# Attention queries projected by token halves, the second half woven with the attention, query loads on SyncE's queue

## Chip, core and metric

The kernel runs on one core of a Trainium2 chip. The metric is the device time of one execution in microseconds (us). PE is TensorE, PEld its weight loads, DVE VectorE, ACT ScalarE, POOL GpSimd and SP SyncE, which here only issues DMAs.

## What is computed

One encoder block over 1024 tokens of width 1024, float32. Both mixers read the same normalised input through one projection; the attention takes its first 768 columns (512 of queries, 128 of keys, 128 of values).

```python
xn = _rmsnorm(h, norm_mix_w[l])
proj = xn @ w_in[l]
q_a, k_a, v_a, qkv_g, z_g, a_g, b_g = jnp.split(proj, SPLIT_POINTS, axis=-1)
attn = _windowed_gqa(q_a, k_a, v_a, band_bias, in_window, attn_sink[l])   # 8 heads, 2 kv heads, window 128
gdn = _gdn_mixer(qkv_g, z_g, a_g, b_g, conv_w[l], gdn_a_log[l], gdn_dt_bias[l], gdn_norm_w[l])
h = h + jnp.concatenate([attn, gdn], axis=-1) @ w_out[l]
hn = _rmsnorm(h, norm_ffn_w[l])
h = h + jnp.square(jax.nn.relu(hn @ w_ffn_in[l])) @ w_ffn_out[l]
return _rmsnorm(h, norm_final_w)
```

Attention works by blocks of 128 queries (`n`, 0 to 7) against the block before, their own and the next. The second mixer is a gated delta rule in both directions, with a triangular inversion per chunk of 128 tokens.

## The kernel before, in words

Every float32 product of the projections is made of three matmuls: weight and input are each split into a rounded part and a remainder (`split`, L119 on ACT and L120 on POOL), and `mm3` (L124 to L126) adds high by high, high by low, low by high. A `gemm` takes 128 weight columns against 512 tokens: 8 slices of the inner dimension, 24 matmuls. The normalised, transposed and split input is held as `xt[0]` (tokens 0 to 511) and `xt[1]` (tokens 512 to 1023), eight tiles of the tag `pg` each. `pg` has 28 buffers, `sc` and `wr` 4, `wh` and `wl` (split weights) 3, `pt` 12; the PSUM tags `psA` and `psB` have 4 banks each. A tile that finds no buffer waits until an earlier one is read for the last time.

Work is written as generators that yield an estimate of what they have issued. `weave` takes the next piece from the stream whose sum of estimates, divided by its weight, is smallest, and so fixes the written order of instructions. The framework then takes that order as priority and lays out the order of each engine at compile time; on the chip each engine runs its own list in order.

First stage (about 90 to 333 us of the profiled execution): `proj_conv` for v, `proj_z` and `proj_attn` are woven with `prep`, `eliminate`, `diag_blocks` and `invert` for its first two steps (0 and 1):

```python
run(weave((chain(self.proj_conv(C_GV, "v"), self.proj_z(), self.proj_attn()), 145.0),
          (chain(self.prep(), self.eliminate(0), self.diag_blocks(0), self.eliminate(1), self.diag_blocks(1),
                 self.invert(tt, (0, 1))), 100.0)))
self.bias_table()
```

At its end `proj_attn` projects the queries: for each of two kv heads it loads 256 columns, and `pair` runs four gemms: the first half of the tokens for two column tiles, then the second half for both. Each result is scaled on DVE (L492), rounded on ACT (L493), its remainder taken on POOL (L494), and both parts are stored to the DRAM scratch `qad` by four DMAs on SP (L498). `bias_table` loads the four bias tiles (L527, SP).

Second stage (about 333 to 570 us): `output`, which begins with `attention`, is woven with `invert` steps 2 and 3 and then two scans of eight steps each:

```python
run(weave((output(), 100.0),
          (chain(self.invert(tt, (2, 3)), self.scan(0, tt[0], w_attn), self.load_wout(0, (2,)),
                 self.scan(1, tt[1], w_gdn)), 95.0)))
```

`attention` has 16 steps (block `n`, kv head). A step makes scores (`attn_scores`, L542 and L543 on PE, L544 on DVE, L556 on ACT, L561 on DVE and POOL), issues the query load for the step two later (`query`, L592, from POOL's queue), and then closes the step two before it: transposes (L571), copies (L573), and after each second step the product with the values (L583, L586) and a store to `mad` (L587, SP). The queries of the first two steps are loaded in `proj_attn`.

`invert` is a chain through POOL (memset of its target, L708), ACT (L712, L721, L742, L753), PE (L718, L728, L732, L751, L759) and DVE (L737, L744, L762), with its input `atd` loaded on SP (L705). `invert` 2 and 3 take one target each from `wh` and `wl`, the others from `pg`. `eliminate(1)` and `diag_blocks(1)` use `sc`; the latter's two tiles are read by all four inversions. Each scan step takes two `sc` tiles, loads `kvd` (L788), `pd` (L790) and, every second step of the first scan, `ktd` and `qtd` (L778) on SP, and makes its products at L795.

Of the kernel before, what the change touches and what calls it, by code (L numbers as in the profile page):

```python
# [9 lines left out]
F32 = mybir.dt.float32  # L10
F32R = mybir.dt.float32r
BF16 = mybir.dt.bfloat16
AF = mybir.ActivationFunctionType
ALU = mybir.AluOpType
AX = mybir.AxisListType

P = 128
# [3 lines left out]
NK = D // P  # L21
HALF = 512
# [32 lines left out]
def weave(*streams):  # L55

    live = [[0.0, i, g, w] for i, (g, w) in enumerate(streams)]
    while live:
        s = min(live, key=lambda e: (e[0], e[1]))
        try:  # L60
            v = next(s[2])
            s[0] += v / s[3]
            yield v
        except StopIteration:
            live.remove(s)
# [12 lines left out]
class Block:  # L78
# [167 lines left out]
    def w_cols(self, w, c0, n):  # L246
        return lambda kh: [(slice(0, n), w[kh * 512:(kh + 1) * 512, c0:c0 + n].rearrange("(k p) c -> p k c", p=P))]

    def split_w(self, raws, view):
        h, l = self.wh((P, NK, P)), self.wl((P, NK, P))  # L250
        for kh in range(2):
            self.split(view(raws[kh]), h[:, 4 * kh:4 * kh + 4, :], l[:, 4 * kh:4 * kh + 4, :])
        return h, l
# [206 lines left out]
    def proj_attn(self):  # L460


        nc = self.nc
        w = self.io["w_in"][0]
        raws = self.load_w(self.w_cols(w, C_AK, 256))
        lo, up = slice(0, 64), slice(64, 128)
        self.kh, self.kl = [self.pg(dt=F32R) for _ in range(2)], [self.pg(dt=F32R) for _ in range(2)]
        for v, o in enumerate((up, lo)):
            nc.vector.tensor_copy(out=self.kl[v][o, :], in_=self.zero[o, :].to_broadcast([64, SEQ]))
        self.va = self.pg((P, NT, P))  # L470
        for i, half, ps in self.pair(raws):
            tok = slice(half * HALF, (half + 1) * HALF)
            t = self.pt()
            nc.vector.tensor_copy(out=t, in_=ps)
            if i == 0:
                swap = self.pt()
                nc.sync.dma_start(out=swap[up, :], in_=t[lo, :])
                nc.sync.dma_start(out=swap[lo, :], in_=t[up, :])
                for v, (r, o) in enumerate(((lo, up), (up, lo))):
                    nc.scalar.copy(out=self.kh[v][r, tok], in_=t[r, :])  # L480
                    nc.scalar.copy(out=self.kh[v][o, tok], in_=swap[o, :])
                    nc.gpsimd.tensor_tensor(out=self.kl[v][r, tok], in0=t[r, :], in1=self.kh[v][r, tok].bitcast(F32),
                                            op=ALU.subtract)
            else:
                pv = self.transposed(t, 0)
                nc.vector.tensor_copy(out=self.va[:, 4 * half:4 * half + 4, :], in_=pv)
            yield 5.2
        for kv in range(2):
            raws = self.load_w(self.w_cols(w, C_AQ + 256 * kv, 256))
            for i, half, ps in self.pair(raws):  # L490
                q, qh = self.pt(), self.pt(dt=F32R)
                nc.vector.tensor_scalar(out=q, in0=ps, scalar1=0.125, scalar2=None, op0=ALU.mult)  # L492
                nc.scalar.copy(out=qh, in_=q)  # L493
                nc.gpsimd.tensor_tensor(out=q, in0=q, in1=qh.bitcast(F32), op=ALU.subtract)  # L494
                for part, t in enumerate((qh.bitcast(F32), q)):
                    o = 64 * (kv ^ part)
                    for g in range(2):
                        nc.sync.dma_start(out=self.qad[kv, 2 * i + g, o:o + 64, half * HALF:(half + 1) * HALF],  # L498
                                          in_=t[64 * g:64 * g + 64, :])
                if i == 1 and half == 0:  # L500
                    self.qs.append(self.query(0, kv))
                yield 5.2


    def bias_rows(self):
# [83 lines left out]
    def query(self, n, kv):  # L589

        q = self.pt((P, 4, P), F32R)
        self.nc.gpsimd.dma_start(out=q, in_=self.qad[kv, :, :, n * P:(n + 1) * P].rearrange("g c t -> c g t").bitcast(F32R))  # L592
        return q

    def attention(self):

        steps = [(n, kv) for n in range(NT) for kv in range(2)]
        qs = self.qs
        open_, pts = [], []

        def close():
            n, kv, tiles, kbs = open_.pop(0)
            pts.append(self.attn_transpose(tiles, kbs))
            yield 1.3
            if kv == 1:
                self.attn_value(n, pts[:], kbs)
                pts.clear()
                yield 2.6

        for i, (n, kv) in enumerate(steps):  # L610
            mk = self.pg if i % 3 == 2 else self.wr
            open_.append((n, kv, *self.attn_scores(n, kv, self.small((P, 4), tag="nm", bufs=12), qs.pop(0), mk)))
            if i + 2 < len(steps):
                qs.append(self.query(*steps[i + 2]))
            yield 1.3
            if len(open_) > 2:
                yield from close()
        while open_:
            yield from close()
# [634 lines left out]
    def phases(self):  # L1254
        nc = self.nc
# [28 lines left out]
        tt = [[None] * 4, [None] * 4]  # L1284
        self.ct, self.ctt = [None, None], [None, None]
        self.kc, self.qc = [None] * 4, [None] * 4
        self.qs = []
        self.wo, self.hnt, self.scanned, self.summed, self.rows = [{}, {}], [None, None], set(), [], {}
        run(weave((chain(self.proj_conv(C_GV, "v"), self.proj_z(), self.proj_attn()), 145.0),
                  (chain(self.prep(), self.eliminate(0), self.diag_blocks(0), self.eliminate(1), self.diag_blocks(1),  # L1290
# [4 lines left out]
        cols, rest = {}, {}  # L1295

        def output():
            yield from self.attention()
            yield from self.out_attn()
            cols[0], rest[0] = self.columns(self.load_w1(0), 1)  # L1300
            out = self.out_all(range(NT - 1, -1, -1))
            while len(self.summed) < 4:
                yield next(out)
            yield from weave((out, 20.0), (self.tokens_second(), 9.0))

        w_attn = {3: self.load_wout(0, (0,)), 5: self.load_wout(0, (1,)), 7: self.load_wout(0, (3,))}
        w_gdn = {1: self.load_wout(1, (0,)), 2: self.load_wout(1, (1, 2)), 4: self.load_wout(1, (3,))}
# [3 lines that stand above are left out]
# [5 lines left out]
        steps = [(n, p) for n in range(ng // 4) for p in SECOND]  # L1316
# [61 lines left out]
```

## Time and profile before

| | |
|---|---|
| median of 3 runs | 1251.35 us (1249.99 to 1251.94) |
| the profiled execution | 1248.56 us |
| its span | 1246.8 us |
| mean granted clock of TensorE | 0.98 |
| busy: PE, DVE, ACT, POOL | 1184.7, 854.8, 620.7, 577.9 us |

All views are of the one profiled execution. Times in them are microseconds from the start of the span. A row of the timeline gives start, duration, engine, source line, operation, the tile written and the tiles read, and in brackets how long the engine had been idle and what ended that. A row of the waits gives who waited for whom, the sum, the number of times and the longest. The granted clock is a share of TensorE's full clock.

### The profile page before, as it was taken

What the parts mean: (1) busy time and instruction counts of PE and PEld (TensorE: products, weight loads), DVE (VectorE), ACT (ScalarE), POOL (GpSimd) and SP (SyncE); (2) the same over time, 40 slices, a digit from 0 to 9 for tenths busy, and PEclk for the clock granted to TensorE, in tenths of its full rate; (3) what the DMA queues carried; (4) which work ended last, traced back from release to release, by engine and by line L of the source; (5) the groups of instructions that cost most, each with busy time, mean ns of one, the idle gap of its engine ahead of it and who ended that gap; (6) DMA issues with size and microseconds to landing.
All of it is one profiled execution on the core that took longest, in us unless ns stands there. A gap on an engine that the chain in (4) does not pass through costs nothing. (4 is left out here: it accounts for less than half of the span.)

```text
span 1246.8 us, 18527 instructions
## 1 busy us (share of the span) xinstructions
PE 1184.7 (95%) x6482; PEld 968.6 (78%) x6482; DVE 854.8 (69%) x1528; ACT 620.7 (50%) x1347; POOL 577.9 (46%) x488
## 2 busy tenths in 40 slices
PE   7999999899789989998899999999999999999997
PEld 5788877778568868877788888888777888888885
DVE  5677667982389986676645453544669797886976
ACT  6455688345485752125464554545545433444343
POOL 5354211352432333244564535535455555655595
PEclk9999999899889999999999999999999999999999
DMA  6134444341855668122234444443688624444333
GB/s 240 52 121 137 114 157 148 132 127 43 228 169 156 185 219 296 60 85 86 84 120 158 145 153 144 150 165 134 226 284 282 230 85 158 152 125 146 98 89 135
DMA packets 121630, 187.62 MB, mean 150 GB/s; under 512 B 11043, under 2 KB 64416, under 8 KB 121537
## 3 DMA queue, kind: packets, MB, share of 16 engines
q1 hardware_dynamic: 96708, 152.58, 37.6%
q10 hardware_dynamic: 16381, 29.67, 6.2%
q0 software_dynamic: 8448, 4.20, 1.8%
q8 instruction: 51, 0.84, 0.3%
q14 instruction: 42, 0.34, 0.1%
HBM read 122.39 MB, written 63.49 MB: 149 GB/s over the span
## 5 line engine op out<-in xcount | busy, mean ns | idle before, releaser
L124 PE MATMUL psA<-pg,wh 128*128 128x512 f32 x416 | 166.4, 401 | 2.1 <-ACT pt L456 2.1
L126 PE MATMUL psA<-pg,wl 128*128 128x512 f32 x416 | 165.7, 398 | 0.0
L125 PE MATMUL psA<-pg,wh 128*128 128x512 f32 x416 | 165.3, 397 | 0.0
L120 POOL TENSOR_TENSOR wl<-wr,wh 128x512 fp32r<-128x512 f32 x44 | 69.4, 1600 | 153.0 <-ACT wh L119 152.9
L1152 DVE TENSOR_TENSOR pg<-pg 128x512 fp32r<-128x512 f32 x112 | 123.1, 1133 | 19.5 <-ACT pg L1151 19.5
L120 POOL TENSOR_TENSOR wh<-wr,wh 128x512 fp32r<-128x512 f32 x32 | 47.7, 1511 | 129.1 <-ACT wh L119 129.1
L125 PE MATMUL psA<-pg,pg 128*128 128x512 f32 x256 | 99.8, 391 | 0.4 <-POOL pg L120 0.4
L124 PE MATMUL psA<-pg,pg 128*128 128x512 f32 x256 | 99.0, 391 | 1.1 <-DVE pg L1197 0.9
L126 PE MATMUL psA<-pg,pg 128*128 128x512 f32 x256 | 99.7, 389 | 0.0
L1069 ACT ACTIVATE pt<-pt 128x512 f32<-128x512 f32 x64 | 40.4, 631 | 117.6 <-DVE pt L1059 117.6
L120 POOL TENSOR_TENSOR pg<-wr,pg 128x512 fp32r<-128x512 f32 x48 | 73.4, 1558 | 50.8 <-ACT pg L119 50.8
L124 PEld LDWEIGHTS psA<-pg,wh 128*128 128x128 f32 x416 | 79.5, 191 | 19.9 <-ACT pt L456 2.4
L125 PEld LDWEIGHTS psA<-pg,wh 128*128 128x128 f32 x416 | 79.4, 191 | 18.4 <-issue 0.9
L126 PEld LDWEIGHTS psA<-pg,wl 128*128 128x128 f32 x416 | 79.4, 191 | 16.9
L1151 ACT CAST pg<-pg 128x512 fp32r<-128x512 f32 x112 | 66.8, 620 | 42.0 <-DMA pg<-sd 30.3
L125 PE MATMUL psB<-pg,pg 128*128 128x512 f32 x192 | 75.0, 391 | 0.8 <-POOL pg L120 0.7
L126 PE MATMUL psB<-pg,pg 128*128 128x512 f32 x192 | 75.0, 390 | 0.3 <-DVE pg L1152 0.3
L124 PE MATMUL psB<-pg,pg 128*128 128x512 f32 x192 | 74.7, 390 | 0.3 <-ACT pg L1151 0.3
L119 ACT CAST wh<-wr 128x512 fp32r<-128x512 f32 x76 | 43.6, 623 | 43.9 <-PE psA L125 24.3
L1059 DVE TENSOR_TENSOR pt<-psB,pt 128x512 f32<-128x512 f32 x39 | 26.9, 690 | 56.0 <-PE psB L126 29.9
L1059 DVE TENSOR_TENSOR pt<-psA,pt 128x512 f32<-128x512 f32 x39 | 26.8, 689 | 54.0 <-PE psA L126 38.8
L124 PEld LDWEIGHTS psA<-pg,pg 128*128 128x128 f32 x256 | 48.0, 188 | 12.7 <-DVE pg L1197 2.2
(385 smaller groups left out, 3303.7 us busy)
## 6 DMA issues: line engine op xcount, KB each, us to landing
sd<-pt ACTq DMA_DIRECT2D x112, 256.0 KB, 2.1
pg<-sd SPq DMA_DIRECT2D x112, 256.0 KB, 2.9
wr<-in_w_ffn_in SPq DMA_DIRECT2D x32, 512.0 KB, 3.7
wr<-in_w_in SPq DMA_DIRECT2D x22, 512.0 KB, 5.4
pg<-in_x SPq DMA_DIRECT2D x16, 512.0 KB, 4.9
wr<-in_w_ffn_out SPq DMA_DIRECT2D x16, 512.0 KB, 5.1
sc<-kvd SPq DMA_DIRECT2D x14, 512.0 KB, 6.4
kvd<-pt SPq DMA_DIRECT2D x16, 256.0 KB, 2.6
```

The lines of the kernel that those rows point to most:

```text
L119: nc.scalar.copy(out=h, in_=raw)
L120: (eng or nc.gpsimd).tensor_tensor(out=l, in0=raw, in1=h.bitcast(F32), op=ALU.subtract)
L124: nc.tensor.matmul(ps, wh, xh, start=first, stop=False, skip_group_check=onto)
L125: nc.tensor.matmul(ps, wh, xl, start=False, stop=False, skip_group_check=onto)
L126: nc.tensor.matmul(ps, wl, xh, start=False, stop=last, skip_group_check=onto)
L1059: self.nc.vector.tensor_tensor(out=out, in0=in0, in1=in1, op=ALU.add)
L1069: self.nc.scalar.activation(out=c, in_=c, func=AF.Relu)
L1151: nc.scalar.copy(out=s[:, 0], in_=raw)
L1152: v.tensor_tensor(out=s[:, 1], in0=raw, in1=s[:, 0].bitcast(F32), op=ALU.subtract)
```

## The change

`proj_attn` now makes only the gemms of the first half of the tokens, for all four column tiles, and keeps the split weights: three pairs in `wh` and `wl`, the fourth in two `sc` buffers. The four gemms of the second half move to a new generator `proj_late`, woven inside `output` with `attention` at weights 30 to 20; `attention` issues no query load of blocks 4 to 7 before `proj_late` has issued all of its stores. The query of block 0 is loaded after both column tiles of its kv head. `query` is issued by SP instead of POOL.

```diff
-    def split_w(self, raws, view):
-        h, l = self.wh((P, NK, P)), self.wl((P, NK, P))
+    def split_w(self, raws, view, tags=None):
+        hi, lo = tags or (self.wh, self.wl)
+        h, l = hi((P, NK, P), F32R), lo((P, NK, P), F32R)
...
+        self.qw = {}
         for kv in range(2):
             raws = self.load_w(self.w_cols(w, C_AQ + 256 * kv, 256))
-            for i, half, ps in self.pair(raws):
-                q, qh = self.pt(), self.pt(dt=F32R)
...
-                if i == 1 and half == 0:
-                    self.qs.append(self.query(0, kv))
+            for i in range(2):
+                tags = (self.sc, self.sc) if kv and i else (self.wh, self.wl)
+                self.qw[kv, i] = self.split_w(raws, lambda r: r[:, :, i * P:(i + 1) * P], tags)
+                self.store_query(kv, i, 0)
                 yield 5.2
+            self.qs.append(self.query(0, kv))
+
+    def store_query(self, kv, i, half):
+        nc = self.nc
+        ps = self.gemm(self.qw[kv, i], self.xt[half], "psA")
+        q, qh = self.pt(), self.pt(dt=F32R)
+        nc.vector.tensor_scalar(out=q, in0=ps, scalar1=0.125, scalar2=None, op0=ALU.mult)
+        nc.scalar.copy(out=qh, in_=q)
+        nc.gpsimd.tensor_tensor(out=q, in0=q, in1=qh.bitcast(F32), op=ALU.subtract)
+        for part, t in enumerate((qh.bitcast(F32), q)):
+            o = 64 * (kv ^ part)
+            for g in range(2):
+                nc.sync.dma_start(out=self.qad[kv, 2 * i + g, o:o + 64, half * HALF:(half + 1) * HALF],
+                                  in_=t[64 * g:64 * g + 64, :])
+
+    def proj_late(self):
+        for kv in range(2):
+            for i in range(2):
+                self.store_query(kv, i, 1)
+                yield 5.2
+        self.late = True
...
     def query(self, n, kv):
         q = self.pt((P, 4, P), F32R)
-        self.nc.gpsimd.dma_start(out=q, in_=self.qad[kv, :, :, n * P:(n + 1) * P].rearrange("g c t -> c g t").bitcast(F32R))
+        self.nc.sync.dma_start(out=q.bitcast(F32), in_=self.qad[kv, :, :, n * P:(n + 1) * P].rearrange("g c t -> c g t"))
         return q
...
             if i + 2 < len(steps):
+                while steps[i + 2][0] * P >= HALF and not self.late:
+                    yield 0.5
                 qs.append(self.query(*steps[i + 2]))
...
-        self.qs = []
+        self.qs, self.late = [], False
...
-            yield from self.attention()
+            yield from weave((self.proj_late(), 30.0), (self.attention(), 20.0))
```

More of the change, by code (lines that the diff above doesn't have):

```diff
@@ L487, in proj_attn @@
             yield 5.2
+        self.qw = {}
         for kv in range(2):
             raws = self.load_w(self.w_cols(w, C_AQ + 256 * kv, 256))
-            for i, half, ps in self.pair(raws):
-                q, qh = self.pt(), self.pt(dt=F32R)
[L492 to L499, printed above, removed]
-                if i == 1 and half == 0:
-                    self.qs.append(self.query(0, kv))
-                yield 5.2
+            for i in range(2):
+                tags = (self.sc, self.sc) if kv and i else (self.wh, self.wl)
+                self.qw[kv, i] = self.split_w(raws, lambda r: r[:, :, i * P:(i + 1) * P], tags)
+                self.store_query(kv, i, 0)
+                yield 5.2
+            self.qs.append(self.query(0, kv))
[17 more added lines that the diff above has]
+        self.late = True
     def bias_rows(self):
```

## The prediction

> **What bounds the kernel now.** I read the page's busy times first, then the busy time of each engine by stage, then the waits of TensorE in the stretch that stands out, and last the order of instructions on the engines that it waits for.
>
> ```profile
> PE 1184.7 (95%) x6482; PEld 968.6 (78%) x6482; DVE 854.8 (69%) x1528; ACT 620.7 (50%) x1347; POOL 577.9 (46%) x488
> 278.70:314.20 35.50, 35.50 (x502) 28.47 (x504) 7.99 (x16) 17.41 (x29) 8.40 (x9) 0.95 0.19 52
> 314.20:333.40 19.20, 14.77 (x114) 12.34 (x113) 5.40 (x9) 5.87 (x10) 6.97 (x6) 0.91 0.80 190
> 333.40:371.60 38.20, 30.00 (x545) 24.15 (x543) 30.36 (x101) 30.34 (x77) 16.56 (x20) 0.82 0.68 193
> 371.60:462.00 90.40, 83.82 (x610) 68.78 (x608) 83.37 (x276) 58.38 (x168) 28.44 (x26) 1.00 0.64 185
> 475.00:640.00 165.00, 154.48 (x801) 130.95 (x800) 104.34 (x220) 57.02 (x132) 72.03 (x66) 0.96 0.31 106
> ```
>
> In the stage rows the columns after the length are the busy time of PE, PEld, DVE, ACT and POOL, then the granted clock, the DMA share and GB/s. PE is busy 95% of the span, so only what empties PE, or slows its clock, can move the end by much. At 278.7 the inversions start; their first two are woven with query gemms until 314.2 and PE has no gap. From 314.2 to 371.6 lie the end of inversion 1, the last two query gemms (done at 333.4), inversions 2 and 3, and the first attention steps: PE idles (19.20 - 14.77) + (38.20 - 30.00) = 12.6 us there, and the clock drops to 0.91 and 0.82. From 371.6 scan and attention run together at full clock; PE (83.82 of 90.40) and DVE (83.37) are about equally full.
>
> The clock in five-microsecond pieces:
>
> ```profile
> 320.00:325.00 5.00, 5.00 (x40) 4.15 (x35) 1.38 (x2) 1.77 (x4) 4.71 (x4) 0.66 0.74 181
> 335.00:340.00 5.00, 1.43 (x65) 1.19 (x65) 2.70 (x6) 4.17 (x6) 4.98 (x6) 0.72 1.12 326
> 340.00:345.00 5.00, 4.90 (x112) 4.52 (x112) 4.21 (x18) 4.93 (x15) 3.04 (x5) 0.60 1.22 323
> 345.00:350.00 5.00, 2.51 (x28) 2.02 (x27) 3.54 (x14) 4.23 (x13) 1.20 (x2) 0.74 0.47 136
> 350.00:355.00 5.00, 5.00 (x26) 4.07 (x26) 2.77 (x11) 3.43 (x10) 0.46 (x1) 0.57 0.28 54
> ```
>
> Busy time times the missing clock is what the slow clock costs: 5.00 x 0.34 = 1.70, 1.43 x 0.28 = 0.40, 4.90 x 0.40 = 1.96, 2.51 x 0.26 = 0.65, 5.00 x 0.43 = 2.15; together 6.9 us, an estimate. So this stretch loses 12.6 + 6.9 = 19.5 us. Its largest waits, and the chain behind the first:
>
> ```profile
> PE psB L759 <- ACT pt L753: 5.0, 2, 4.4
> PE psB L718 <- DMA pg<-atd: 3.4, 2, 1.7
> PE psB L751 <- DVE pt L744: 3.1, 2, 2.5
> ...
> POOL pt L592 <- DMA pg<-biasd: 12.4, 2, 8.7
> ...
> 314.43 1.00 POOL L592 DMA_DIRECT2D pt<-qad  x1 [3.67 <-DMA pg<-biasd]
> 315.44 0.97 POOL L708 MEMSET pg<- 128x1024 f32 x1
> ...
> 316.44 2.52 ACT L712 COPY pg<-sc 32x256 f32<-32x256 f32 x4 [7.11 <-POOL pg L708]
> 318.98 0.58 ACT L753 COPY pt<-psB 128x512 f32<-128x512 f32 x1
> ...
> 319.62 1.59 PE L759 MATMUL psB<-pg,pt 64*64 64x64 f32 x32 [4.43 <-ACT pt L753]
> ```
>
> Read upwards: PE sits idle 4.43 us for L753, which stands in ACT's order behind the copies L712, which waited 7.11 us for the memset L708, which stood in POOL's order behind the query load L592. POOL waits in order: 12.4 us in two waits at L592. The load's releaser is named as the bias load; I take it to be the stores to `qad` that the query reads, queued on SP around those loads.
>
> **The change, part by part.** The sum is made against the profiled execution, 1248.56 us with its 1246.8 us span; the median of the three runs, 1251.35, is 2.8 us higher, and I subtract the same saving from it.
>
> Four gemms move. Their pace and what goes with each:
>
> ```profile
> 231.11 0.39 PE L124 MATMUL psA<-pg,wh 128*128 128x512 f32 x1
> ...
> 231.79 0.39 PE L124 MATMUL psA<-pg,wh 128*128 128x512 f32 x1
> ...
> 333.02 0.39 PE L126 MATMUL psA<-pg,wl 128*128 128x512 f32 x1
> 333.25 0.28 PE L542 MATMUL psA<-pg,pt 128*128 128x256 f32 x1
> ...
> 371.62 1.16 PE L795 MATMUL psB<-sc,pg 128*128 128x128 f32 x8
> ...
> L494 POOL TENSOR_TENSOR pt<-pt,pt 128x512 f32<-128x512 f32 x8 | 10.1, 1283 | 12.0 <-issue 7.8 <-ACT pt L493 4.2
> L492 DVE TENSOR_SCALAR pt<-psA 128x512 f32<-128x512 f32 x8 | 5.2, 686 | 10.2 <-PE psA L126 10.2
> L493 ACT CAST pt<-pt 128x512 fp32r<-128x512 f32 x8 | 4.7, 618 | 11.9 <-DVE pt L492 11.8
> L498 SPq DMA_DIRECT2D qad<-pt x32: 445/568/1675, 296.5 to 339.5; - x32
> L592 POOL DMA_DIRECT2D pt<-qad x16 | 12.8, 803 | 12.7 <-DMA pg<-biasd 12.4 <-PE psA L583 0.3
> ```
>
> Three matmuls per 0.68 us, 24 per gemm: 5.4 us, so 21.8 us of PE work leaves the end of the first stage and enters the second; now the last query matmul starts at 333.02, the first score at 333.25 and the first scan product at 371.62. PE does the same work in all. With each go one DVE, ACT and POOL instruction (four times 0.69, 0.62 and 1.28 us: 2.7, 2.5 and 5.1 us) and four SP stores (16 x 0.57 = 9.1 us). Cover: they may run anywhere before 371.6, where DVE is busy only 7.99 of 35.5 and 5.40 of 19.2 us; I cost them at nothing. Without that cover, behind the full DVE after 371.6, it is 2.7 us.
>
> What it can give: attention needs only the first halves for its first eight steps, so it can start up to 21.8 us earlier, beside inversions 1 to 3, and the late gemms, which wait for nothing but a PSUM bank, can fill PE where it idles. Ceiling: 19.5 us. Floor: nothing, if the same waits reappear. Taking the waits singly: the 4.43 us with the 1.70 us of slow clock behind it has the POOL wait as its cause, and that goes with the load's move to SP: 6.1 us. Next in line there is the buffer of that memset: `pg` is full at that point, and the eight tiles of the first half's x are freed by the fourth early gemm instead of the sixth, so it comes earlier, not later. Of the remaining 8.2 us idle and 5.2 us of clock I take 6 us, a little under half: the late gemms cover what lies between ready pieces, but each engine still works in a fixed order made beforehand, and the loads of `atd` for inversion 2 must still come. Then 1.6 us back: the moved 21.8 us will not run gapless but as the stage after 371.6 does, (90.40 - 83.82) / 90.40 = 7% idle. Sum: 6.1 + 6 - 1.6 = 10.5 us.
>
> The query loads leave POOL (16 x 0.80 = 12.8 us of its issue time, and its two waits) and take SP issue time, 16 x 0.57 = 9.1 us by the nearest row, the stores. SP now does the waiting: behind a query load that waits for its stores (2.5 us to land) stand loads of `atd`, of the scan and stores of `mad`.
>
> ```profile
> SPq L587 <- DVE pt L586: 21.3, 1, 21.3
> ...
> qad<-pt SPq DMA_DIRECT2D x32, 128.0 KB, 2.5
> pt<-qad POOLq DMA_DIRECT2D x16, 256.0 KB, 4.3
> pt<-pd SPq DMA_DIRECT2D x16, 256.0 KB, 3.9
> pg<-qtd SPq DMA_DIRECT2D x4, 512.0 KB, 10.0
> ```
>
> SP already stands up to 21.3 us at one store of `mad` without PE missing a load, so a few more waits of 2.5 us are hidden by loads issued ahead. Bounds: nothing, or two waits of 2.5 us in the path (the first two queries), 5 us; taken nothing, since later queries are issued two attention steps ahead. An SP load of the same size lands in 3.9 us against 4.3 us from POOL: no loss. A load right behind others lands late (`qtd`, issued behind `ktd`, 10.0 us); for a first query that would be 10.0 - 4.3 = 5.7 us more, which the late gemms (21.8 us) would cover. [...]
>
> Held buffers: the split weights stay until the late gemms (all three `wh` and `wl`, two of four `sc`), and the second half's x, eight of 28 `pg`. Inversion 2 takes a `wh`, free after the first late gemm; the scan's second step takes the two `sc`, free after the last.
>
> **The rivals.**
>
> First, the order hardly changes: the late gemms are ready at once and get used up right behind the first halves. Then only the POOL wait goes: 6.1 us, 1245.2.
>
> Second, given back: DVE, 92% busy from 371.6, sets the pace of attention and scan, and what PE gains before is waited for later. 1251, no change. Against it: attention started earlier also brings DVE work into the stretch where DVE idles.
>
> Third, slower: the two `sc` hold up the scan.
>
> ```profile
> 365.07 0.38 SPq L788 DMA_DIRECT2D sc<-kvd  x1
> ...
> 379.40 0.33 SPq L587 DMA_DIRECT2D mad<-pt  x1
> ...
> 395.61 0.32 SPq L587 DMA_DIRECT2D mad<-pt  x1
> ...
> L795 PE MATMUL psB<-sc,pt x128: 270/275/377, 375.2 to 561.8; 128*128 128x128 f32 x128
> ```
>
> The load for the scan's second step is issued at 365.07. If the last late gemm ends later than that, the scan waits. In the written order the gemm stands behind four attention steps of 16.2 / 2 = 8.1 us (from store to store of `mad`): 333.4 - 21.8 + 21.8 + 4 x 8.1 = 366, just at the point. If it slips by one more pair of steps, the scan, which runs until 561.8 at 11.9 us a step, is 16.2 us late, and after 475 PE has little else (10.5 us idle in 165) to do meanwhile. Less the 6.1 us of POOL: 10 us slower, 1261. Smaller mishaps of the same sign, SP waits of 2 x 2.5 us in the path with nothing gained, give 1256.
>
> **How the numbers follow.** Forecast (gaps filled, 10.5 us): 0.52, 1241, its own range 1234 to 1247. Order unchanged, 1245: 0.18. Given back, 1251: 0.12. Slower, 1256 to 1261: 0.18. About 0.2% (2.5 us) is what a measurement of this kernel can tell from no change. Faster 0.70, same 0.12, slower 0.18. The range reaches below to the ceiling of 19.5 us (1232), above into the slower case: 1231 to 1257, which leaves out some 5 in 100 below and 12 above.
>
> **What would show it.** Right: no wait of POOL at the query load, the memset of inversion 1 and the 4.43 us wait at L759 gone or moved; first scores before 320 instead of 333; late gemms between scores and inversion pieces; granted clock near 1.00 from 315 to 355; first scan product (371.62 now) before 365. Wrong: all query gemms still in one block; PE waits in the 330s and 340s as large as before; SP waiting long at a query load with `atd` or `kvd` loads behind it; the load of the scan's second step waiting for a late gemm; more DVE waits after 371.

## The result and the profile after

The changed kernel takes 1277.64 us (median of 4 runs, 1274.91 to 1279.67) against 1250.67 us of the kernel before in the same comparison (4 runs, 1248.10 to 1251.94): ratio 1.0228, 95% interval 1.0210 to 1.0247. It is 27 us slower. The forecast was 1241 in a range of 1231 to 1257, so the sign was wrong and the time lies past even the slower rival, 1261. The profiled execution took 1277.4 us, its span 1275.2 (before: 1248.56 and 1246.8): 28.4 us more span.

The page's busy times, after:

```profile
PE 1188.7 (93%) x6482; PEld 970.7 (76%) x6482; DVE 852.5 (67%) x1528; ACT 620.0 (49%) x1347; POOL 567.7 (45%) x472
```

PE runs the same 6482 matmuls and is busy 4.0 us longer (1188.7 - 1184.7); the other 24 us are idle time of PE. POOL has lost its 16 query loads and 10.2 us. To find the place I cut both traces at the same events: start of the inversions, first scan product, last scan product, first transpose of the tokens for the stage behind the attention, last of these transposes. The columns are those of the prediction's stage rows. After:

```profile
279.20:360.00 80.80, 61.21 (x1058) 50.43 (x1058) 32.23 (x93) 43.44 (x88) 21.08 (x25) 0.79 0.43 124
360.00:535.90 175.90, 159.43 (x1071) 132.51 (x1067) 143.43 (x470) 85.48 (x261) 48.45 (x39) 1.00 0.59 188
535.90:604.10 68.20, 58.35 (x262) 47.60 (x260) 28.70 (x41) 12.64 (x25) 20.26 (x20) 0.95 0.20 66
604.10:651.00 46.90, 38.73 (x188) 32.41 (x189) 29.22 (x44) 20.89 (x39) 19.65 (x20) 0.93 0.19 68
```

Before, at the same events:

```profile
278.70:371.60 92.90, 80.27 (x1154) 64.95 (x1154) 43.76 (x126) 53.62 (x116) 31.94 (x35) 0.89 0.52 139
371.60:561.80 190.20, 180.26 (x1166) 152.21 (x1163) 152.98 (x463) 81.08 (x243) 62.30 (x52) 0.99 0.54 169
561.80:579.90 18.10, 14.43 (x70) 11.63 (x68) 9.24 (x15) 7.66 (x18) 7.98 (x11) 0.99 0.35 117
579.90:621.20 41.30, 37.34 (x188) 31.20 (x189) 29.95 (x44) 20.74 (x37) 19.84 (x20) 0.95 0.22 77
```

Length less PE's busy time is its idle time. Stage by stage, after against before: 19.6 against 12.6, 16.5 against 9.9, 9.9 against 3.7, 8.2 against 4.0 us. That is 23.9 us more idle; PE's busy time over the four rows grows by 5.4 us (317.7 against 312.3, with 2579 and 2578 matmuls), at granted clocks of 0.79, 1.00, 0.95 and 0.93 against 0.89, 0.99, 0.99 and 0.95. Together 29.3 us: the whole of the loss lies in these four stretches, and each of them loses.

The third row shows what has changed: between the end of the scans and the transposes lie 68.2 us instead of 18.1. The scan's products, after (number, durations in ns, first and last start):

```profile
L814 PE MATMUL psB<-sc,pg x320: 270/275/377, 360.0 to 535.2; 128*128 128x128 f32 x160
L814 PE MATMUL psB<-sc,pt x128: 270/275/377, 367.2 to 535.9; 128*128 128x128 f32 x128
```

The last start was 561.8 before; now it is 535.9. The last store of the attention to `mad` went the other way. From the timelines, after and then before:

```profile
502.46 0.38 SPq L604 DMA_DIRECT2D mad<-pt  x1
```

```profile
463.43 0.32 SPq L587 DMA_DIRECT2D mad<-pt  x1
```

So the scan ends 25.9 us earlier and the attention 39.0 us later. Both still have to be done before the end of the stage, and when the scan is over PE has only the output products and their preparation left. What it waits for from 475 to 670, after, and from 475 to 640, before:

```profile
PE psA L927 <- DVE wr L924: 10.5, 3, 4.3
PE psB L207 <- DVE pg L203: 3.7, 1, 3.7
```

```profile
PE psB L207 <- DVE pg L203: 3.7, 1, 3.7
...
PE psA L908 <- DVE wr L905: 1.0, 2, 0.7
```

L924 (L905 before) is the last DVE step of `out_gdn`, which prepares a chunk of the scan's output for the output product; L927 transposes it. That wait grew from 1.0 to 10.5 us.

### The profile page after: what moved, and what is told of

The parts are those of the page before. It is cut to its first block, busy times and chain, and to the rows that moved or that the text cites. A ratio compares the mean times of both kernels' runs of the same rounds, so it can differ in the third digit from the quotient of the medians.

```text
span 1275.2 us, 18506 instructions
## 1 busy us (share of the span) xinstructions
PE 1188.7 (93%) x6482; PEld 970.7 (76%) x6482; DVE 852.5 (67%) x1528; ACT 620.0 (49%) x1347; POOL 567.7 (45%) x472
## 4 chain that ended last, share of the span: by engine, by line
PE 50%; DVE 11%; DMA 5%; issue 5%; POOL 2%; ACT 1%; SPq 0%; POOLq 0%; ACTq 0%; DVEq 0%
PE psA L124 8%; PE psA L125 8%; PE psA L126 7%; PE psB L124 7%; PE psB L126 7%; PE psB L125 7%; PE psB L814 3%; DMA pg<-sd 2%; PE psA L600 1%; DMA sd<-pt 1%; DVE pg L1171 1%; DVE pt L1180 1%; PE psA L588 1%; DMA pg<-in_w_out 1%; DVE wr L561 1%
## 5 line engine op out<-in xcount | busy, mean ns | idle before, releaser
L124 PE MATMUL psA<-pg,wh 128*128 128x512 f32 x400 | 159.7, 400 | 2.2 <-ACT pt L457 2.2
L126 PE MATMUL psA<-pg,wl 128*128 128x512 f32 x400 | 159.2, 398 | 0.0
L125 PE MATMUL psA<-pg,wh 128*128 128x512 f32 x400 | 158.3, 396 | 0.0
L1171 DVE TENSOR_TENSOR pg<-pg 128x512 fp32r<-128x512 f32 x112 | 123.9, 1141 | 16.5 <-ACT pg L1170 16.5
L120 POOL TENSOR_TENSOR wh<-wr,wh 128x512 fp32r<-128x512 f32 x32 | 48.2, 1524 | 127.8 <-ACT wh L119 127.8
L125 PE MATMUL psA<-pg,pg 128*128 128x512 f32 x256 | 99.9, 392 | 0.4 <-POOL pg L120 0.3
L124 PEld LDWEIGHTS psA<-pg,wh 128*128 128x128 f32 x400 | 76.2, 190 | 19.1 <-ACT pt L457 2.4
L125 PEld LDWEIGHTS psA<-pg,wh 128*128 128x128 f32 x400 | 76.2, 190 | 17.5 <-issue 0.9
L126 PEld LDWEIGHTS psA<-pg,wl 128*128 128x128 f32 x400 | 76.1, 190 | 16.3
L125 PE MATMUL psB<-pg,pg 128*128 128x512 f32 x192 | 75.3, 392 | 2.4 <-POOL pg L120 2.3
L1078 DVE TENSOR_TENSOR pt<-psA,pt 128x512 f32<-128x512 f32 x39 | 26.8, 689 | 51.3 <-PE psA L126 36.0
L124 PEld LDWEIGHTS psA<-pg,pg 128*128 128x128 f32 x256 | 48.2, 188 | 12.7 <-DVE pg L1216 2.2
```

What stands on the lines that cost most here:

```text
L120: (eng or nc.gpsimd).tensor_tensor(out=l, in0=raw, in1=h.bitcast(F32), op=ALU.subtract)
L124: nc.tensor.matmul(ps, wh, xh, start=first, stop=False, skip_group_check=onto)
L125: nc.tensor.matmul(ps, wh, xl, start=False, stop=False, skip_group_check=onto)
L126: nc.tensor.matmul(ps, wl, xh, start=False, stop=last, skip_group_check=onto)
L1078: self.nc.vector.tensor_tensor(out=out, in0=in0, in1=in1, op=ALU.add)
L1171: v.tensor_tensor(out=s[:, 1], in0=raw, in1=s[:, 0].bitcast(F32), op=ALU.subtract)
```

## The experiments

Three theories stood against each other. A, the order: the late gemms yield 4 x 5.2 = 20.8 units inside `output`, and `weave` charges them to the stream that carries the attention, so the scan, at 95 to 100 against that stream, runs ahead of the attention. B, the query loads stand in SP's order and hold it up. C, the late gemms hold buffers that others need. Line numbers are those of the kernel before in the experiments built on it (e1, e3, e8, e10, e11, e12), of the changed kernel in the others.

**B alone: e1_sp_query.** The kernel before with one line changed.

```diff
-        self.nc.gpsimd.dma_start(out=q, in_=self.qad[...].bitcast(F32R))
+        self.nc.sync.dma_start(out=q.bitcast(F32), in_=self.qad[...])
```

> The kernel before with one part of the change: the query loads are issued by SP instead of POOL, nothing else. Theory A (the place in the weave: the late gemms stand in the attention's stream and put it behind the scan) expects little here: 1245 to 1255. Theory B (query loads in SP's order) expects most of the 27 us: 1265 to 1277, with long waits for the query tile on PE. Theory C (weights and second-half x held in their buffers) expects no change, 1248 to 1253.

1252.01 us against 1249.77, ratio 1.0024 (1.0008 to 1.0039). B doesn't make the 27 us. PE's waits from 278 to 373 tell about the first term of the prediction:

```profile
PE psB L718 <- DMA pg<-atd: 8.8, 2, 8.5
...
PE psB L759 <- ACT pt L753: 0.7, 1, 0.7
```

The wait at L759 was 5.0 us and is nearly gone, as forecast, but the wait for the load of `atd` at L718 grew from 3.4 to 8.8 us. The query loads on SP did not make that load late: it is issued at 330.91 instead of 332.72. PE is done with the first scores at 326.94 instead of 334.75 and waits for a load that comes hardly earlier. Up to the first transpose of the tokens e1 is still 3.6 us ahead (576.24 against 579.85). Behind it the lead is lost: the wait for the last DVE step of `out_gdn` (L905) sums to 5.3 us instead of 1.0.

**A alone: e3_share_only.** The kernel before with an empty stream that yields what the late gemms yield. Not one instruction is added, removed or moved to another engine; only the written order differs.

```diff
-            yield from self.attention()
+            yield from weave((iter([5.2] * 4), 30.0), (self.attention(), 20.0))
```

> The kernel before with no instruction moved or added: only the order is changed, by weaving a stream that yields 4 x 5.2 and issues nothing into the output stream beside the attention, at 30 to 20 as in the changed kernel. Theory A expects what the changed kernel loses after 377 us, 4.9 + 8.7 + 5.5 = 19 us: 1265 to 1273, with the scan done some 25 us before the last attention step's neighbours and waits of PE for out_gdn's DVE multiply of about 10 us. Theories B and C expect no change: 1248 to 1253.

1274.79 us, ratio 1.0198 (1.0175 to 1.0221), a little above what A expected: 25 of the 27 us without the change's instructions. Its stages, cut as above:

```profile
278.90:368.00 89.10, 69.91 (x1098) 57.77 (x1098) 36.59 (x95) 45.06 (x90) 28.02 (x31) 0.87 0.54 146
368.00:533.20 165.20, 150.06 (x1031) 124.71 (x1027) 142.51 (x468) 84.76 (x259) 53.49 (x46) 1.00 0.60 179
533.20:601.10 67.90, 58.06 (x262) 47.40 (x260) 28.71 (x41) 12.64 (x25) 20.29 (x20) 0.95 0.21 66
601.10:649.40 48.30, 40.45 (x188) 33.37 (x189) 29.25 (x44) 20.86 (x39) 19.65 (x20) 0.89 0.19 66
```

Idle 19.2, 15.1, 9.8 and 7.9 us, together 52.0 against 54.1 in the changed kernel and 30.2 before: the pattern of the changed kernel, the 68 us behind the scan included.

**The share given back: e4_own_stream and e5_late_in_stage1.** Both are the changed kernel, queries on SP and weights held, with the late gemms not charged to the attention. In e4 they are a third stream of the outer weave, in e5 they stand at the end of the first stage's stream.

```diff
-            yield from weave((self.proj_late(), 30.0), (self.attention(), 20.0))
+            yield from self.attention()
...
# e4:
-                         self.scan(1, tt[1], w_gdn)), 95.0)))
+                         self.scan(1, tt[1], w_gdn)), 95.0), (self.proj_late(), 150.0)))
# e5, instead:
-        run(weave((chain(self.proj_conv(C_GV, "v"), self.proj_z(), self.proj_attn()), 145.0),
+        run(weave((chain(self.proj_conv(C_GV, "v"), self.proj_z(), self.proj_attn(), self.proj_late()), 145.0),
```

> The changed kernel with the late gemms as a third stream of the outer weave (weight 150), so that attention and scan keep their shares of before; buffers held and query loads on SP as in the change. Theory A expects the 19 us after 377 back, and what is lost before it (8 us) at most: 1246 to 1259. Theories B and C expect no gain against the change: 1272 to 1280.

> The changed kernel with the late gemms issued at the end of the first stage, behind the early ones, and attention alone in its stream: the order of halves, the buffers and the SP query loads of the change without its weaving. Theory A expects no loss: 1243 to 1254. Theory B expects 1265 to 1277. Theory C expects little loss, since the buffers come free some 22 us later at most: 1250 to 1262.

e4: 1249.62 us, 0.9998 (0.9982 to 1.0013). e5: 1249.19 us, 0.9999 (0.9985 to 1.0012). With the share restored the loss is gone in both; e4 holds the split weights among the inversions as the change does, so C and B together cost nothing net in this order that can be measured. But e4 gains nothing either, although its late gemms lie among the inversions. The stretch up to the first scan product, e4:

```profile
278.30:372.30 94.00, 79.28 (x1154) 63.22 (x1154) 44.33 (x126) 53.12 (x116) 26.68 (x29) 0.89 0.45 126
```

e5, the same stretch and the transposes of the tokens:

```profile
279.20:366.50 87.30, 77.64 (x1155) 62.52 (x1155) 43.41 (x126) 54.05 (x115) 26.37 (x29) 0.92 0.54 155
...
574.20:622.40 48.20, 41.31 (x189) 34.87 (x189) 29.17 (x44) 20.94 (x39) 19.68 (x20) 0.85 0.19 66
```

e4 leaves 14.7 us idle where the kernel before left 12.6. e5 makes the stretch 5.6 us shorter (87.3 against 92.9), so here is a gain, and it is still there at the first token transpose, 574.2 against 579.9. Then 6.9 us are given back: the last row is 48.2 us instead of 41.3. Of these, 2.9 us are idle time of PE and 4.0 us longer busy time, at a granted clock of 0.85 instead of 0.95. The waits of e5 from 475 to 660 name the place; the first summed to 1.0 us in the kernel before, the second was there already:

```profile
PE psA L927 <- DVE wr L924: 4.7, 3, 4.1
PE psB L207 <- DVE pg L203: 3.7, 1, 3.7
```

The last `out_gdn` finishes late, as in the changed kernel and in e1.

**The query back on POOL, and a slower scan: e2_pool_query and e6_scan_slower.** Both start from the changed kernel.

```diff
# e2: the line of query() as in the kernel before
# e6:
-                         self.scan(1, tt[1], w_gdn)), 95.0)))
+                         self.scan(1, tt[1], w_gdn)), 72.0)))
```

> The changed kernel with one part undone: the query loads are issued by POOL again. Theory A (the late gemms' place in the attention's stream puts the attention behind the scan) expects the change's time, 1272 to 1280, less what the first queries cost on SP (a wait of 6.3 us of PE in the 320s), plus POOL's waits of before. Theory B (queries on SP) expects most of the loss back: 1250 to 1260.

> The changed kernel with one number changed: the weight of the stream of inversions and scan is 72 instead of 95, so that attention and scan stand to each other again about as before (62.4 units of attention and 20.8 of late gemms against the same scan). Theory A expects most of the loss back: 1250 to 1262, what remains being the first 90 us after the inversions start. A theory that the held buffers or the mixing of three kinds of work cost the time expects 1270 or more.

e2: 1273.43 us against 1251.78, 1.0176 (1.0145 to 1.0207): in the changed order the query loads on SP cost some 4 us by the medians and 6.5 by the two ratios, which come from two sets of runs, while in the old order e1 was 2 us slower. e6: 1263.23 us, 1.0095 (1.0061 to 1.0128), about half of the loss back. Its scan now ends behind where the kernel before had it; these products start for the last time at 571.2 instead of 561.3:

```profile
L814 PE MATMUL psB<-sc,pg x320: 270/275/421, 358.9 to 571.2; 128*128 128x128 f32 x160
```

One weight doesn't restore the old order. My reading, which no run isolates, is that it slows the scan as long as it lasts, while the late gemms displaced the attention once, at the start.

**The tail: e7_stage1_ready4 and e8_before_ready4.** `out_all` keeps at most three chunks prepared by `out_gdn`. e8 is the kernel before, e7 is e5, both with four from the fourth chunk on, so that the last preparation is written earlier.

```diff
-            while len(ready) < 3 and n + len(ready) < len(chunks) and chunks[n + len(ready)] in self.scanned:
+            while len(ready) < (4 if n > 2 else 3) and n + len(ready) < len(chunks) and chunks[n + len(ready)] in self.scanned:
```

> The kernel with the late gemms at the end of the first stage, and the last chunks of the output mixer prepared four ahead instead of three (from the third chunk on), so that the last one's squares on ACT stand ahead of the norms. The trace of the former showed 6 us gained up to the token transposes and 5 to 6 us lost behind them, at a wait of 4.05 us for the last chunk's multiply on DVE. If that is the place of the loss: 1240 to 1246. If the gain up to there was only a trace's chance: 1248 to 1252.

> The kernel before with the same preparation four ahead and nothing else: tells how much of the former's gain is this alone. The kernel before has no wait for the last chunk's multiply, but 3.7 us for the norm's first row there, which the output gemms now cover: 1245 to 1250.

e7: 1233.45 us, 0.9862 (0.9841 to 0.9883), faster than both kernels. e8: 1240.47 us, 0.9915 (0.9889 to 0.9942). Both came out below what was expected of them. PE's waits of e7 from 475 to 660:

```profile
PE psA L927 <- DVE wr L924: 2.4, 3, 1.9
...
PE psB L207 <- DVE sc L203: 0.2, 1, 0.2
```

The waits at L927 halve (4.7 to 2.4 us) and the 3.7 us ahead of the token transposes, which every kernel with three has, are gone. With this the 5.6 us that e5 won earlier are kept: e7 is 7.0 us below e8, measured in the same set of runs.

**Crossed: e9_own_stream_ready4, e10_sp_query_ready4, e11_scan_later_ready4, e12_share_only_ready4.** These are e4, e1, e8 with the scan's weight 82, and e3, the tail's edit in each.

> The changed kernel with the late gemms as a stream of their own, between the inversions, and the last chunks prepared four ahead. To be set against the kernel with the late gemms behind the early ones (1233.5 with the same preparation). If late gemms between the inversions fill PE's gaps, as I predicted: 1226 to 1231. If they fill nothing and hold the first inversions' length at that of before, as the trace of the own stream without the preparation has it (21.4 us idle and slow clock in that stretch, 21.3 before, 15.0 with the late gemms in stage one): 1238 to 1242.

> The kernel before with query loads on SP and the last chunks prepared four ahead. Splits the 7 us between 1240.5 (preparation alone) and 1233.5 (with halves and SP loads): if they come from POOL's waits at the query load going away, 1235 to 1238 here, since the SP query alone was 3.6 us earlier up to the transposes; if all from the order of halves, 1240.

> The kernel before with the last chunks prepared four ahead and the scan's stream at weight 82 instead of 95: the attention is put ahead of the scan, the opposite of what the change does. If what counts is that attention and scan stay beside each other to the end, it costs here too: 1245 to 1260. If only an early scan is bad: 1236 to 1242.

> The kernel before with the empty stream beside the attention (order alone, as in the share-only run) and the last chunks prepared four ahead. Tells how much of the share's 25 us is the wait for the last chunk's multiply (about 5.5 us by the share-only trace) and how much the order of attention and scan itself: 1255 to 1261 against 1240.5.

e9: 1242.86 us, 0.9949 (0.9931 to 0.9966). e10: 1240.17, 0.9938 (0.9920 to 0.9956). e11: 1244.61, 0.9966 (0.9948 to 0.9984). e12: 1260.12, 1.0104 (1.0070 to 1.0137). These four were run in another set than e7 and e8, so a difference between the sets is given by the medians and by the ratios. e9 falls short of what gap filling called for: with the tail mended, late gemms among the inversions are no better than no change of the projection at all (e8). e10 lies within 3 us of e8 either way, so SP's queue alone is neither the source of e7's lead nor a cost here; the 7 us of e7 come with the order of the halves inside the first stage. Whether that order would give them with the loads on POOL was not run. e12 keeps a loss of 20 us against e8 by the medians (1260.12 - 1240.47) and 24 by the ratios, so the share keeps most of its price. Its tail is only half mended: the 3.7 us ahead of the token transposes are gone, but the wait for `out_gdn` still sums to 8.0 us, 10.5 in e3. e11 came between the two expectations: moving the scan later costs 4 us by the medians, 6 by the ratios. The scan's products of e11 and of e12:

```profile
L795 PE MATMUL psB<-sc,pt x128: 270/275/421, 379.8 to 568.4; 128*128 128x128 f32 x128
```

```profile
L795 PE MATMUL psB<-sc,pt x128: 270/275/377, 374.4 to 535.0; 128*128 128x128 f32 x128
```

e8 ends them at 561.8, like the kernel before. So 6.6 us later cost 4 to 6 us, and 26.8 us earlier cost 20 to 24 us: the old share was the best of the ones tried. That is some 0.6 to 1 us for each microsecond of shift, an estimate from these two points and no rule: e2's scan ends 37.4 us early (524.4), and e2 loses 22 us, less than the change.

## Why the prediction was wrong

**The step that failed** is a term that the sum does not have. The prediction took the late gemms as PE work of the same size in another place and priced what they do to PE's gaps: 6.1 + 6 - 1.6 us. It had the attention start up to 21.8 us earlier; its first score does start 12 us earlier (321.17 instead of 333.25), but its last store comes 39 us later. The sum did not price the yields: 20.8 units charged to `output` at a ratio of 100 to 95 put the attention behind the scan, and that order alone costs 25 us (e3). The numbers to see it stood in the code: the yields, and the weights of the two weaves. It also needed the question of what is left when one of two streams ends first. Of the signs that were to show it right, some came true in the slower kernel: no POOL wait at the query load, first scan product at 360.0 (before 365). These signs speak of the stretch ahead of the scan, where only 7 of the 24 us of new idle time lie.

**"Slower: the two `sc` hold up the scan."** This rival had the sign but the opposite direction: the scan was expected to end 16.2 us late and ended 25.9 us early, and the attention, which the prediction had starting earlier, ended 39 us later. The last late gemm does end behind the point named there. From PE's timeline, after:

```profile
360.04 1.16 PE L814 MATMUL psB<-sc,pg 128*128 128x128 f32 x8
...
376.52 0.39 PE L126 MATMUL psA<-pg,sc 128*128 128x512 f32 x1
```

At 376.5 us it still reads its `sc` weights, but by then the scan is under way (first product 360.0), and e4, which holds the same weights, lost nothing.

**"Ceiling 19.5 us", of which 6 us by late gemms in the gaps.** The stretch to the first scan product got shorter (80.8 against 92.9 us), but because work left it, with 7 us more idle time: it holds 1058 matmuls instead of 1154, and of the 96 that left, 48 belong to the last two late gemms and 48 to the attention. Two gaps of over 6 us stand in it. PE's waits from 279 to 377, after:

```profile
PE psB L778 <- ACT pt L772: 6.8, 2, 6.1
PE psA L559 <- DMA pt<-qad: 6.3, 1, 6.3
PE psB L770 <- DVE pt L763: 6.2, 6, 2.6
```

And the timeline behind the first two (rows of several engines, in order of time):

```profile
308.97 0.96 POOL L727 MEMSET wh<- 128x1024 f32 x1 [1.71 <-PE psA L125]
309.96 2.56 ACT L731 COPY wh<-pg 32x256 f32<-32x256 f32 x4 [4.12 <-POOL wh L727]
312.53 2.51 ACT L731 COPY wl<-pg 32x256 f32<-32x256 f32 x4
315.06 2.50 ACT L731 COPY pg<-sc 32x256 f32<-32x256 f32 x4
317.59 0.58 ACT L772 COPY pt<-psB 128x512 f32<-128x512 f32 x1
318.20 1.14 ACT L505 CAST pt<-pt 128x512 fp32r<-128x512 f32 x2
318.23 1.98 PE L778 MATMUL psB<-pg,pt 64*64 64x64 f32 x32 [6.14 <-ACT pt L772]
318.84 5.99 SPq L510 DMA_DIRECT2D qad<-pt  x8
326.66 0.36 SPq L609 DMA_DIRECT2D pt<-qad  x1
329.57 0.56 PE L559 MATMUL psA<-pg,pt 128*128 128x256 f32 x1 [6.28 <-DMA pt<-qad]
```

**"6.1 us: the POOL wait goes."** It went: no query load stands on POOL. But the same PE matmul of inversion 1 (L759 before, L778 now) waits 6.14 us instead of 4.43, because its ACT copy L772 stands behind twelve copies for inversions 2 and 3 (2.56 + 2.51 + 2.50 us). They could not begin before POOL's memset of `wh`, and that memset waited for the first late gemm (L125) to release the buffer. "It comes earlier, not later" was said of `pg`; the held `wh` was named in the next paragraph and given no price. In e1 the time went into the wait for `atd`. The gain of a wait removed depends on what stands next in each engine's list, and three orders gave three answers: 8.8 us of waiting for `atd` (e1), 6.14 us for ACT (the change), and a stretch that is 5.6 us shorter (e5).

**"SP waits taken nothing, bounds 0 to 5 us."** A query load on SP at 326.66 stands behind eight stores to `qad`, and the score that needs it waits 6.28 us. That wait is not SP's price. The eight stores are those of the early gemms of the second kv head, which this load reads, and POOL's queue did not spare it the wait: in e2, where POOL issues it, the same score waits 4.1 us. The stores are late because their data are: the two casts L505 (the rounding, L493 before) stand on ACT right behind L772, at 318.20, so both gaps hang on the same twelve copies. Two of the waits of SP, 279 to 377, after:

```profile
...
SPq L510 <- ACT pt L505: 7.7, 4, 5.3
SPq L609 <- DMA qad<-pt: 1.6, 1, 1.6
```

The 5.3 us belong to the stores in front, 1.6 us to the load itself. The net price of SP is 4 to 6.5 us in the changed order (e2) and 2 us or nothing in the old one (e1; e10 against e8): at the upper bound or a little above it, not at the value taken. What it is made of was not taken apart. For a first query right behind other loads the prediction named 5.7 us more, covered by the late gemms: the first one on SP, issued at 312.45 behind three loads of `atd`, landed in 6.4 us against 4.0 from POOL before, and no wait of PE hangs on it. Over all query loads the medians are 4.4 us from SP after the change and 4.3 us from POOL before.

**Late gemms that "fill gaps".** Neither of the two gaps after the change holds a late gemm: the first one ends at 309.1, the second starts at 345.3, behind both instructions that PE waited with (L778 at 318.23, L559 at 329.57). `weave`, from which each engine's list is made, goes by estimates; my reading is that a late gemm fills a gap only where the list has it ahead of the instruction that waits. e4 and e9 wrote the late gemms among the inversions with the shares kept, and gained nothing by it.

**What stays open.** That the order costs most of the 24 us of idle time is shown by e3, which has 22 of them without the change's instructions; which placement each microsecond in the second stretch (16.5 against 9.9 us) hangs on was not isolated. Nor was it tried to keep the late gemms inside `output` with yields of zero. Why some orders put the last `out_gdn` late (e1, e2, e3, e5, e6, the change) and others do not (the kernel before, e4) was not taken apart; writing it earlier mends it in e7 and only in part in e12.

## What to carry to other kernels

When a piece of work moves into another stream of a weave, price its yields as well as its instructions: they push back whatever shares that stream, and an empty stream with the same yields measures that by itself. Where two streams must both end before the next stage, ask which ends first and what PE has left to do then. A gain won early (5.6 us in e5) is only kept if the stage that follows has its inputs prepared early enough; look there before calling the change useless.

## What the runs showed of the hardware

Around two gaps of 6 us the granted clock stood at half from 314 to 344 us. Five-microsecond pieces, after:

```profile
310.00:315.00 5.00, 1.17 (x32) 1.00 (x30) 2.11 (x4) 4.92 (x8) 1.70 (x2) 0.87 0.89 290
315.00:320.00 5.00, 1.77 (x32) 1.77 (x32) 0.00 (x0) 4.23 (x8) 1.10 (x1) 0.50 0.77 259
320.00:325.00 5.00, 3.29 (x76) 2.81 (x74) 3.93 (x13) 0.56 (x2) 1.94 (x4) 0.50 0.71 164
325.00:330.00 5.00, 0.42 (x2) 0.46 (x3) 0.00 (x0) 4.92 (x11) 1.26 (x1) 0.50 0.59 163
330.00:335.00 5.00, 2.87 (x104) 2.51 (x103) 4.43 (x18) 3.42 (x15) 1.01 (x1) 0.50 0.67 199
335.00:340.00 5.00, 3.10 (x46) 2.78 (x48) 3.13 (x9) 1.11 (x2) 2.46 (x4) 0.50 0.01 3
340.00:345.00 5.00, 5.00 (x112) 4.54 (x114) 2.51 (x6) 2.36 (x5) 0.04 (x1) 0.56 0.02 3
345.00:350.00 5.00, 5.00 (x47) 4.08 (x39) 0.00 (x0) 0.00 (x0) 0.00 (x0) 1.00 0.00 0
```

It falls to 0.50 within the first gap (312.1 to 318.2): in pieces of one microsecond it is 1.00 up to 313, 0.86 in the next and 0.50 from 314. It comes back to 1.00 only behind a piece in which PE is busy 5.00 of 5.00 us; the pieces with 3.10 and 3.29 us busy didn't bring it back. Between the two gaps PE works without a pause from 318.23 to 323.29, 5.06 us (1.77 and 3.29 in the rows), and the clock stays at 0.50. From 339.28 it works without a pause again; in pieces of one microsecond the clock is 0.50 up to 344, 0.78 in the next and 1.00 from 345. So this stretch paid twice: from 315 to 340 PE idles for 13.55 of 25 us, and its 11.45 us of work run at half clock, where a score matmul (128x256) mostly took 0.41 us, against 0.28 us in the kernel before at a clock of 1.00.
